# Two PSUM banks for the projections of the first part and of the last tail, and two sets of weight buffers in that tail

## Chip, core and metric

The kernel runs on one core of a Trainium2 chip. The metric is the device time of one execution in microseconds. Three executions of the kernel before gave 3626.5, 3629.08 and 3631.28 us; the median is 3629.08 us.

## The reference

One layer of a hybrid decoder for 1024 prompt tokens and 32 sample tokens, width 1024, in float32:

```python
z = rms_norm(x) @ W_in                   # 28 column chunks of 128: q,k,v of A; q,f,i,g of B
oa = dilated_attention(qa, ka, va)       # group A: 8 heads x 64
ob = hgrn2_chunked(qb, logf, kb, ib, s0) # group B: 4 heads x 128, gated
x += concat[rms_norm(oa), ob * silu(gb)] @ W_out
x += cross_attention(rms_norm(x), mk, mv, w_cq, w_co)   # 256 memory tokens
q = rms_norm(x) @ w_pq                   # 8 heads x 2 halves x 128: 16 column chunks
v1, i1 = top_k(q1 @ k1.T, 16); v2, i2 = top_k(q2 @ k2.T, 16)
sc, ci = top_k(all sums v1 + v2, 16);  e = i1[..] * 128 + i2[..];  g = softmax(sc)
a = gelu(x . peer_u[e]);  x += (g * a) @ peer_v[e]       # 16384 experts, 16 per head
y = rms_norm(x)
```

## The kernel before

**Products.** A float32 product is made of three matmuls of split operands (`mm3`, L201 to L203: high by high, high by low, low by high). `project` takes one PSUM bank, runs `mm3` over the input chunks into it and evacuates it. Weights come through `load_w`: two buffers for a projection with 1024 inputs (`kc` 8), one for one with 512, from a tag with three buffers. The first use of a weight splits it and stores it to DRAM (`wd_*`); later parts load the split form, 512 KB to a buffer, from the SP queue.

**Parts.** The 8 prompt tiles of 128 tokens and the sample tile (number 8) are worked through in three parts: tiles 0, 1, 2, then 3, 4 and the sample, then 5, 6, 7. Part 0 also carries the sample's 32 columns through its projections (416 columns). Each part has `z` (28 projections with `w_in`, each 24 matmuls into bank `z`, weights in `wz`), the attention and the recurrence that use them, and a `tail`: `w_out` (8 chunks), `w_cq` (4), cross attention, `w_co` (8, of 512 inputs) and `w_pq` (16), each `w_pq` chunk followed by the products with the expert keys (L674) and `top16` on VectorE (L917 to L921). The tails of parts 0 and 1 use the tag set "T" (weights `wt`, bank `y`), run beside the next part's middle, and are not changed. The tail of part 2 uses the set "Z" (weights `wz`, bank `z`), and runs beside `gates` 3 and 4, which build the dense gate matrix (L1024 to L1036).

**Experts.** Tiles 0 to 4 go through all 16384 experts densely: 128 iterations, each with the product of activations and the `u` block (bank `a`, L201 to L203), gelu (L1088), the product with the gates `gt` (L1090), its split (L170) and the products with the `v` block (L1098 to L1100). Inputs of the first iteration are `xh` and `xl` (eight loads, L1047), `gt` (L1064) and `u`. Tiles 5, 6, 7 and the sample gather their expert rows instead: GpSimd issues an indirect DMA per row (L1183), VectorE makes the dot product (L1190) or adds the row (L1201). Their indices come out of `select_tile` (L932 to L988) for the three tiles of part 2, called here a pick; the picks stand in the program between the first dense iterations. At the end stand the final norms (L1138 to L1153), the sample's last, which loads the sample's sum back (`u<-accd`).

**Order.** The Tile framework's scheduler makes one static order for each engine from the program, its buffers and its own estimate of durations; each engine runs its order strictly. A change of a buffer's name can thus move instructions anywhere on all engines. Where tiles live is decided by the allocation: the second dense gate buffers (`gt`, its third slot) lie on the same SBUF bytes as the `wt` buffers.

Of the kernel before, what the change touches and what calls it, by code (L numbers as in the profile page):

```python
# [64 lines left out]
def _body(tc, nc, ctx, A, O):  # L65
    V, S, PE, G, SP, ANY = nc.vector, nc.scalar, nc.tensor, nc.gpsimd, nc.sync, nc.any
# [23 lines left out]
    def T(p, shape, dt=F32, tag=None, bufs=None):  # L90
        seq[0] += 1
        kw = {} if bufs is None else {"bufs": bufs}
        if p is wk:
            p = wl if tag in LONG else wr if tag == "res" else we
        return p.tile(shape, dt, name=f"{tag}_{seq[0]}", tag=tag, **kw)

    def bank(tag="m"):
        return T(ps, [128, 512], F32, BANKS[tag], PB.get(BANKS[tag], 1))
# [69 lines left out]
    def split(hi, lo, src):  # L168
        S.copy(hi, src)  # L169
        V.tensor_tensor(lo, src, hi, op=ALU.subtract)  # L170
# [10 lines left out]
    def load_w(name, c, kc, tag, keep=True):  # L181
        out = []
        for i in range(kc // 4):
            w = T(wk, [128, 2, 4, 128], F32R, tag, 3)
            if (name, c, i) in wd:
                SP.dma_start(w.bitcast(F32), wd[name, c, i])
            else:
                raw = T(wk, [128, 4, 128], F32, "raw", 2)
                SP.dma_start(raw, A[name][c][:, 4 * i : 4 * i + 4])
                split(w[:, 0], w[:, 1], raw)  # L190
                if keep:
                    wd[name, c, i] = T(dr, [128, 2, 4, 128], F32, f"wd_{name}_{c}_{i}")
                    SP.dma_start(wd[name, c, i], w.bitcast(F32))
            out.append((w[:, 0], w[:, 1]))
        return out

    def mm3(out, w, x, kc, sl):
        xhi, xlo = x
        for c in range(kc):
            whi, wlo = (y[:, c % 4] for y in w[c // 4])  # L200
            PE.matmul(out, lhsT=whi, rhs=xhi[:, c, sl], start=c == 0, stop=False)  # L201
            PE.matmul(out, lhsT=whi, rhs=xlo[:, c, sl], start=False, stop=False)  # L202
            ins = PE.matmul(out, lhsT=wlo, rhs=xhi[:, c, sl], start=False, stop=c == kc - 1)  # L203
        return ins
# [18 lines left out]
    def hi_lo(g):  # L223
        return T(wk, [128, 8, g["xw"]], F32R, g["hi"]), T(wk, [128, 8, g["xw"]], F32R, g["lo"])

    def norm_T(src, n, g, bc, x, own=False):
        for c in range(8):
            s = src(c)
            t = s if own else T(wk, [128, WQ], F32, "t", TB)[:, :n]
            V.scalar_tensor_tensor(t, s, col(par, g + c), bc[:, :n], op0=ALU.mult, op1=ALU.mult)  # L230
            split(x[0][:, c, :n], x[1][:, c, :n], t)
        return x

    def gain_T(src, n, g, x):
        for c in range(8):
            hi, lo = (y[:, c, :n] for y in x)
            S.activation(hi, src(c), AF.Copy, scale=col(par, g + c))
            V.scalar_tensor_tensor(lo, src(c), col(par, g + c), hi, op0=ALU.mult, op1=ALU.subtract)
        return x
# [58 lines left out]
    def part(pi):  # L298
# [12 lines left out]
        WZP, N, NT = width(zt), width(th), len(th)  # L311
# [6 lines left out]
        h = []  # L318
# [17 lines left out]
        def project(w, x, kc, n, evac, tag):  # L336
            p = bank(tag)[:, :n]
            ins = mm3(p, w, x, kc, slice(0, n))
            if pi:
                anchors.append(ins)  # L340
            evac(p)

        def z(chunk, dst, fn=None):
            w = load_w("w_in", chunk, 8, "wz")

            def evac(p):
                if fn is None:
                    ANY.tensor_copy(dst, p[:, :NP])
                else:
                    S.activation(dst, p[:, :NP], fn)  # L350
                if first:
                    ANY.tensor_copy(zs[:, chunk], p[:, NP:])

            project(w, h, 8, WZP, evac, "z")

        def turn(dst, src, tag="m"):
            p = bank(tag)
# [4 lines left out]
        def z_some(c, group):  # L362
            r = {}
            for k, tag in group:
                t = T(wk, [128, 1024 if tag == "kT" else WT], F32, tag)
                r[tag] = t
                o = c0 if tag == "kT" else 0
                if o:
                    SP.dma_start(t[:, :c0], kdr[c][:, :c0])
                z(4 * k + c, t[:, o : o + NP], {"hq": AF.Silu, "gs": AF.Silu, "f": AF.Sigmoid}.get(tag))  # L370
            return r
# [148 lines left out]
        def tail(g):  # L520
            g = TAGS[g]
            tb = lambda k: bank(g["bank"] + k)
            tq = lambda k: T(wk, [128, g["qw"]], F32, g["q"][k])
            tw = lambda shape, dt=F32: T(g["pool"], shape, dt, g["tw"], 2)
            c2 = lambda shape, dt=F32: T(g["pool"], shape, dt, g["c2"], PTB if g["c2"] == "PT" else 2)
            put = lambda name, kc, x, evac: [
                project(load_w(name, c, kc, g["w"]), x, kc, N, lambda p: evac(c, p), g["bank"] + "y")
                for c in range(A[name].shape[0])]
            if smp:
                p = tb("m")  # L530
# [6 lines left out]
            y = hi_lo(g)  # L537
# [26 lines left out]
            if smp:  # L564
                p = tb("m")
# [17 lines left out]
            for j in range(NB):  # L583
                sl = slice(j * 128, (j + 1) * 128)
                po = tb("o")
                for hp2 in range(2):
# [16 lines left out]
                    p = tb("m")  # L603
# [17 lines left out]
            if smp or any(t in DENSE for t, o, rows in th):  # L621
                bc = bcast(r, th, g["bank"] + "m", g["bc"])
                h3 = norm_T(lambda c: xr[:, c, :N], N, G_FFN, bc, hi_lo(g))
                rs = None
            else:
                h3 = gain_T(lambda c: xr[:, c, :N], N, G_FFN, hi_lo(g))
# [9 lines left out]
            for j, (t, o, rows) in enumerate(th):  # L636
                xn = tw([128, 1024])
                for q in range(2):
                    p = tb("m")
# [16 lines left out]
            o = 0  # L656
# [5 lines left out]
            for jc in range(16):  # L662
                if jc % 8 == 0:
                    keys = tw([128, 8, 128])
                    SP.dma_start(keys, A["keys"][:, jc : jc + 8])
                    if smp:
                        sc4 = T(wk, [128, 2, 128], F32, "sc4")
                q = tq(jc % 2)
                project(load_w("w_pq", jc, 8, g["w"]), h3, 8, N, lambda p: ANY.tensor_copy(q[:, :N], p),
                        g["bank"] + "y")  # L670
                p = tb("m")
                for j, (t, o, rows) in enumerate(th):
                    r0 = 32 * (jc // 2 % 4) if t == 8 else 0
                    PE.matmul(p[r0 : r0 + rows, j * 128 : (j + 1) * 128], lhsT=q[:, o : o + rows], rhs=keys[:, jc % 8],  # L674
                              start=True, stop=True)
                sco = tq(2 + jc % 2)[:, : NB * 128].rearrange("p (j n) -> p j n", n=128)
                ANY.tensor_copy(sco, p[:, :NP].rearrange("p (i n) -> p i n", n=128))
                for j in range(NB):
                    top16(sco[:, j], lists[j][0][:, jc], lists[j][1][:, jc])
                if smp:  # L680
                    r0 = 32 * (jc // 2 % 4)
                    ANY.tensor_copy(sc4[r0 : r0 + 32, jc % 2], p[r0 : r0 + 32, NP : NP + 128])
                    if jc % 8 == 7:
                        for s in range(2):
                            k = jc // 8 * 2 + s
                            top16(sc4[:, s], lists[NB][0][:, k], lists[NB][1][:, k])
                if jc % 4 == 3:
                    yield
# [227 lines left out]
    def top16(s, v, i):  # L916
        V.max(v[:, 0:8], s)  # L917
        V.max_index(i[:, 0:8], v[:, 0:8], s)
        V.match_replace(s, v[:, 0:8], s, -3e38)
        V.max(v[:, 8:16], s)  # L920
        V.max_index(i[:, 8:16], v[:, 8:16], s)  # L921
# [308 lines left out]
    def seq_of(*fs):  # L1230
        for f in fs:
# [3 lines left out]
            else:  # L1235
                yield

    p = [part(i) for i in range(3)]

    def ahead(q):  # L1240
# [13 lines left out]
    with tc.tile_pool(name="dn", bufs=1, reuse_waits="tile") as dn, \  # L1254
            tc.tile_pool(name="dps", bufs=1, space=PSUM, reuse_waits="tile") as dps:
        work = dense(dv, dn, dps)
        for f in picks:
            next(work)
            f()
        late.close()  # L1260
        more = ctx.enter_context(tc.tile_pool(name="more", bufs=1, side="right", reuse_waits="tile"))
        for _ in work:
            pass
        for t in [t for part in PARTS for t in sorted(part, reverse=True) if t not in DENSE]:
            gather_tile(t)
        finish_sample(dn, dps)
# [103 lines left out]
```

## Time and profile before

| | |
|---|---|
| median of three executions | 3629.08 us |
| the profiled execution's own time | 3627.68 us |
| its span in the trace | 3625.8 us |
| mean granted TensorE clock | 0.977 |
| moved by DMA | 1007.82 MB, mean 278 GB/s |

The profiled execution is 1.4 us under the median; 1.9 us of it lie outside the span. The first 1650 us or so are parts and tails, then come some 90 us in which the last tail ends and the dense stage starts, then the dense stage to about 3580 us, and the final norms. Engine shares over all of that say little on one place; the stretches below are read apart.

### The profile page before, as it was taken

The page shows a single profiled execution, that of the slowest core. Times are in us where ns is not written, and L with a number is a line of the kernel's source. Part 1 is how long each engine was busy: PE and PEld are TensorE (multiplying, and loading weights), DVE is VectorE, ACT ScalarE, POOL GpSimd, SP SyncE. Part 2 cuts the span into 40 slices and gives each one's busy share as a digit, 9 for nine tenths or more (in the row PEclk, how much of TensorE's full clock was granted, in tenths as well). Part 3 has the DMA queues.
Part 4 walks back from the last instruction along what each step waited for, and adds up shares of the span by engine and source line. Part 5 has one row for each costly group of instructions (what it writes and reads, how often), then busy time and mean ns, then how long its engine had stood idle before and what let it go on. Part 6 is the DMA issues. An engine that isn't in the chain of part 4 may idle for free.

```text
span 3625.8 us, 52725 instructions
## 1 busy us (share of the span) xinstructions
PE 3373.7 (93%) x19343; PEld 2912.4 (80%) x19343; DVE 2634.7 (73%) x5868; ACT 1220.6 (34%) x2282; POOL 1112.5 (31%) x871
## 2 busy tenths in 40 slices
PE   5999999999999889887799999999999999999994
PEld 4886776677887788777788998999888898988893
DVE  4443333243885687897888878988888898888997
ACT  4544344344434443431242222222222222222221
POOL 0000000000000000021316644656566565565555
PEclk9999999999999999898999999999999999999997
DMA  7667777656655485499659988999999999999998
GB/s 243 230 226 248 239 247 240 202 181 220 210 192 201 179 293 209 150 338 344 229 169 348 341 291 286 364 351 337 340 335 351 345 333 342 337 343 332 329 328 296
DMA packets 408514, 1007.82 MB, mean 278 GB/s; under 512 B 43968, under 2 KB 168896, under 8 KB 406848
## 3 DMA queue, kind: packets, MB, share of 16 engines
q1 hardware_dynamic: 288448, 568.20, 45.6%
q0 software_dynamic: 119808, 436.26, 33.0%
q8 instruction: 152, 2.49, 0.3%
q14 instruction: 106, 0.87, 0.1%
HBM read 866.01 MB, written 138.31 MB: 277 GB/s over the span
## 4 chain that ended last, share of the span: by engine, by line
PE 71%; DVE 10%; DMA 9%; issue 4%; ACT 3%; POOL 1%; SPq 1%; POOLq 0%; DVEq 0%; ACTq 0%
PE a L201 7%; PE a L203 7%; PE a L202 7%; PE y L1098 4%; PE y L1099 4%; PE y L1100 4%; PE z L201 4%; PE z L202 3%; PE z L203 3%; PE yr L1098 3%; PE yr L1099 2%; PE yr L1100 2%; PE y L201 2%; PE y L202 2%; PE y L203 2%
## 5 line engine op out<-in xcount | busy, mean ns | idle before, releaser
L1183 POOL DMA_INDIRECT row<-in_peer_u,ix x416 | 534.6, 1285 | 635.9 <-DVE dots L1190 347.6
L1183 POOL DMA_INDIRECT row<-in_peer_v,ix x416 | 543.1, 1306 | 412.1 <-DVE ha L1201 266.5
L201 PE MATMUL a<-xh,u 128*128 128x320 f32 x2048 | 636.8, 311 | 21.2 <-ACT w L1088 18.0
L203 PE MATMUL a<-xh,u 128*128 128x320 f32 x2048 | 634.5, 310 | 0.7 <-DVE u L170 0.7
L202 PE MATMUL a<-xl,u 128*128 128x320 f32 x2048 | 634.1, 310 | 0.0
L1201 DVE SCALAR_TENSOR_TENSOR ha<-row,dots,ha 128x1024 f32<-128x1024 f32 x416 | 533.0, 1281 | 22.2 <-DMA row<-in_peer_v,ix 17.8
L1190 DVE CUSTOM_DVE_ANT_0 row<-row,ha 128x1024 f32<-128x1024 f32 x416 | 497.9, 1221 | 39.5 <-DMA row<-in_peer_u,ix 39.5
L210 POOL TENSOR_TENSOR rs_r<-rs_m,mhalf 128x3 f32<-128x3 f32 (+2 forms) x25 | 23.4, 944 | 1369.7 <-DVE rs_m L208 1250.2
L1088 ACT ACTIVATE w<-a 128x320 f32<-128x320 f32 x256 | 111.6, 436 | 937.3 <-PE a L203 917.1
L201 PEld LDWEIGHTS a<-xh,u 128*128 128x128 f32 x2048 | 385.6, 188 | 40.5 <-ACT w L1088 25.8
L202 PEld LDWEIGHTS a<-xl,u 128*128 128x128 f32 x2048 | 385.7, 188 | 8.8
L203 PEld LDWEIGHTS a<-xh,u 128*128 128x128 f32 x2048 | 385.5, 188 | 2.8 <-DVE u L170 1.0
L201 PE MATMUL z<-zhi,wz 128*128 128x384 f32 (+2 forms) x928 | 330.4, 356 | 43.0 <-DMA wz<-wd_w_pq 16.2
L202 PE MATMUL z<-zlo,wz 128*128 128x384 f32 (+2 forms) x928 | 316.8, 341 | 3.4 <-DVE zlo L170 1.9
L203 PE MATMUL z<-zhi,wz 128*128 128x384 f32 (+2 forms) x928 | 314.0, 338 | 0.0
L1099 PE MATMUL y<-v,w 128*128 128x512 f32 x768 | 294.6, 392 | 0.0
L1098 PE MATMUL y<-v,w 128*128 128x512 f32 x768 | 269.6, 393 | 12.6 <-ACT v L169 11.2
L1100 PE MATMUL y<-v,w 128*128 128x512 f32 x768 | 264.5, 391 | 1.3 <-DVE w L170 1.2
L201 PEld LDWEIGHTS z<-zhi,wz 128*128 128x128 f32 x928 | 181.0, 195 | 87.3 <-issue 21.7
L1098 PE MATMUL yr<-v,w 128*128 128x512 f32 x512 | 201.8, 394 | 13.5 <-DVE ys L1127 11.7
L169 ACT CAST w<-w 128x320 fp32r<-128x320 f32 x256 | 117.8, 460 | 259.0 <-DVE w L1090 258.5
L1100 PE MATMUL yr<-v,w 128*128 128x512 f32 x512 | 199.9, 390 | 0.7 <-DVE w L170 0.7
(470 smaller groups left out, 6685.2 us busy)
## 6 DMA issues: line engine op xcount, KB each, us to landing
u<-in_uT SPq DMA_DIRECT2D x128, 512.0 KB, 7.0
v<-in_peer_v SPq DMA_DIRECT2D x128, 512.0 KB, 7.6
wz<-wd_w_in SPq DMA_DIRECT2D x112, 512.0 KB, 4.3
gt<-gtall SPq DMA_DIRECT2D x124, 320.0 KB, 10.8
wd_w_in<-wz SPq DMA_DIRECT2D x56, 512.0 KB, 3.2
gtall<-sg SPq DMA_DIRECT2D x34, 512.0 KB, 4.1
wd_w_pq<-wt SPq DMA_DIRECT2D x32, 512.0 KB, 3.1
wt<-wd_w_pq SPq DMA_DIRECT2D x32, 512.0 KB, 4.5
```

The lines of the kernel that those rows point to most:

```text
L169: S.copy(hi, src)
L201: PE.matmul(out, lhsT=whi, rhs=xhi[:, c, sl], start=c == 0, stop=False)
L202: PE.matmul(out, lhsT=whi, rhs=xlo[:, c, sl], start=False, stop=False)
L203: ins = PE.matmul(out, lhsT=wlo, rhs=xhi[:, c, sl], start=False, stop=c == kc - 1)
L210: G.tensor_tensor(r, m, mhalf[:, :n], op=ALU.pow)
L1088: S.activation(ga[:, lo:hi], pa, AF.Gelu)
L1098: PE.matmul(o, lhsT=wh[:, sl], rhs=vh[:, ds], start=start and q == 0, stop=False)
L1099: PE.matmul(o, lhsT=wh[:, sl], rhs=vl[:, ds], start=False, stop=False)
L1100: PE.matmul(o, lhsT=wl[:, sl], rhs=vh[:, ds], start=False, stop=stop and q == len(ws) - 1)
L1183: G.indirect_dma_start(out=row, out_offset=None, in_=tab, in_offset=bass.IndirectOffsetOnAxis(ap=col(ix, j), axis=0))
L1190: V.tensor_tensor_reduce(row, row, hn, 1.0, 0.0, op0=ALU.mult, op1=ALU.add, accum_out=col(dots, j))
L1201: V.scalar_tensor_tensor(acc, row, col(dots, j), acc, op0=ALU.mult, op1=ALU.add)
```

## The change

The 28 projections of part 0 take turns between bank `z` and bank `x` (which the kernel maps to the physical bank `g`, also used by the sample's attention). In the tail of part 2, odd chunks of `w_out`, `w_cq`, `w_co` and `w_pq` go to bank `o` instead of `z`, and their weights to the three buffers of `wt` instead of the three of `wz`. `wt` also serves part 1's tail, which ends first.

```diff
+        zn = [0]
+
         def z(chunk, dst, fn=None):
             w = load_w("w_in", chunk, 8, "wz")
...
-            project(w, h, 8, WZP, evac, "z")
+            zn[0] += 1
+            project(w, h, 8, WZP, evac, "z" if pi or zn[0] % 2 else "x")
...
+            by = lambda c: "o" if pi == 2 and c % 2 else g["bank"] + "y"
+            wtag = lambda c: "wt" if pi == 2 and c % 2 else g["w"]
             put = lambda name, kc, x, evac: [
-                project(load_w(name, c, kc, g["w"]), x, kc, N, lambda p: evac(c, p), g["bank"] + "y")
+                project(load_w(name, c, kc, wtag(c)), x, kc, N, lambda p: evac(c, p), by(c))
                 for c in range(A[name].shape[0])]
...
-                project(load_w("w_pq", jc, 8, g["w"]), h3, 8, N, lambda p: ANY.tensor_copy(q[:, :N], p),
-                        g["bank"] + "y")
+                project(load_w("w_pq", jc, 8, wtag(jc)), h3, 8, N, lambda p: ANY.tensor_copy(q[:, :N], p),
+                        by(jc))
```

Lines behind the first edit stand 2 or 3 further down in the changed kernel, those behind the tail's edits 5: L1090 is L1095 there.

What the order shows. TensorE, first projections of part 0 (`z_266` is the first chunk's bank, `g_308` the second's; a piece of the difference):

```order
 L203 MATMUL z_266<-zhi_201,wz_252 128x416
+L201 MATMUL g_308<-zhi_201,wz_294 128x416
+L202 MATMUL g_308<-zlo_202,wz_294 128x416
+L203 MATMUL g_308<-zhi_201,wz_294 128x416
+L201 MATMUL g_308<-zhi_201,wz_294 128x416
+L202 MATMUL g_308<-zlo_202,wz_294 128x416
+L203 MATMUL g_308<-zhi_201,wz_294 128x416
 L201 MATMUL z_266<-zhi_201,wz_252 128x416
+L201 MATMUL g_308<-zhi_201,wz_294 128x416
 L202 MATMUL z_266<-zlo_202,wz_252 128x416
```

The second chunk's matmuls now stand between the first's, which come as the pieces of the normed input do; before they followed the first's evacuation. The third begins where it did.

The SP queue ahead of the dense stage, before (`wz` are the last `w_pq` weights, `xh`, `xl`, `gt`, `u` the dense inputs):

```order
L1047 DMA xh_15700<-h3x_65_163 128x1280
L186 DMA wz_15220<-wd_w_pq_1_1475_6874 128x1024
L1047 DMA xl_15701<-h3x_66_164 128x1280
L1047 DMA xh_15700<-h3x_65_163 128x1280
L1047 DMA xl_15701<-h3x_66_164 128x1280
L174 DMA u_15732<-in_uT 128x1024
L186 DMA wz_15272<-wd_w_pq_0_1483_6931 128x1024
L1047 DMA xh_15700<-h3x_65_163 128x1280
L1064 DMA gt_15720<-gtall_165 128x5x64
L186 DMA wz_15274<-wd_w_pq_1_1486_6938 128x1024
```

And now, from the last of the eight activation loads on:

```order
L1052 DMA xh_15700<-h3x_65_163 128x1280
L1052 DMA xl_15701<-h3x_66_164 128x1280
L1052 DMA xh_15700<-h3x_65_163 128x1280
L1052 DMA xl_15701<-h3x_66_164 128x1280
L1069 DMA gt_15720<-gtall_165 128x5x64 x4
L1069 DMA gt_15725<-gtall_165 128x5x128 x4
L1069 DMA gt_15730<-gtall_165 128x5x128
L174 DMA u_15732<-in_uT 128x1024
L1069 DMA gt_15730<-gtall_165 128x5x128 x3
```

Seventeen of the 32 `w_pq` weight loads stood behind the first `xh` load before, and three `u` loads ahead of the last weights; now all 32 weights are ahead of the eight `xh` and `xl` loads, and every `u` load comes after. The four `gt_15725` loads go to the bytes of `wt` and wait for the last projection's matmuls, and the first `u` is queued behind them.

VectorE at the end, before, from the last sum of the dense stage on (`ys`, L1127; `ha_31808` is the last gathered tile, a row for each gathered expert):

```order
L1127 TENSOR_TENSOR ys_3269_15718<-ys_3269_15718,yr_29565 128x512
L1201 SCALAR_TENSOR_TENSOR ha_31808<-row_32160,dots_31423,ha_31808 128x1024
L1201 SCALAR_TENSOR_TENSOR ha_31808<-row_32163,dots_31423,ha_31808 128x1024
L1201 SCALAR_TENSOR_TENSOR ha_31808<-row_32166,dots_31423,ha_31808 128x1024
L1201 SCALAR_TENSOR_TENSOR ha_31808<-row_32169,dots_31423,ha_31808 128x1024
L1201 SCALAR_TENSOR_TENSOR ha_31808<-row_32172,dots_31423,ha_31808 128x1024
L1152 SCALAR_TENSOR_TENSOR u_29589<-u_29589,fst_29593,u_29598 128x1024
```

And now:

```order
L1132 TENSOR_TENSOR ys_3269_15718<-ys_3269_15718,yr_29565 128x512
L1153 TENSOR_SCALAR fst_29593<-fst_29593 128x1
L1206 SCALAR_TENSOR_TENSOR ha_31808<-row_32187,dots_31423,ha_31808 128x1024
L1206 SCALAR_TENSOR_TENSOR ha_31808<-row_32190,dots_31423,ha_31808 128x1024
L1206 SCALAR_TENSOR_TENSOR ha_31808<-row_32193,dots_31423,ha_31808 128x1024
L1157 SCALAR_TENSOR_TENSOR u_29589<-u_29589,fst_29593,u_29598 128x1024
```

Behind the last `ys` there were twelve gathered rows (to `row_32193`), and there are three now. At the start of the dense stage the move is the other way: the first product with the gates (L1090, now L1095) stood ahead of nearly all of the first pick's instructions on VectorE, and now stands behind all but a few of them; the split of the first `u` block (L170) stands behind most of that pick too.

## Rows read from the trace of the kernel before

**Rows 1.** The page, busy time, share of the span and instructions of each engine.

```profile
PE 3373.7 (93%) x19343; PEld 2912.4 (80%) x19343; DVE 2634.7 (73%) x5868; ACT 1220.6 (34%) x2282; POOL 1112.5 (31%) x871
```

**Rows 2.** Stretches: length, busy time of each engine, PEclk, DMA share, GB/s.

```profile
26.00:48.00 22.00, 11.08 (x24) 7.11 (x24) 12.35 (x25) 6.96 (x13) 0.00 (x0) 1.00 0.59 188
...
700.00:1100.00 400.00, 392.25 (x2287) 318.96 (x2285) 248.50 (x1063) 167.39 (x284) 5.26 (x6) 0.98 0.60 201
...
1420.00:1580.00 160.00, 133.05 (x847) 124.09 (x846) 140.89 (x441) 71.25 (x155) 12.66 (x12) 0.90 0.54 193
1580.00:1643.00 63.00, 52.23 (x347) 48.98 (x346) 61.99 (x137) 22.65 (x49) 14.10 (x12) 0.92 0.97 355
1643.00:1680.00 37.00, 27.95 (x147) 25.81 (x147) 32.51 (x176) 7.00 (x13) 5.62 (x6) 0.86 1.01 385
1680.00:1735.00 55.00, 41.19 (x214) 37.46 (x212) 36.99 (x180) 9.40 (x18) 8.56 (x10) 0.91 0.90 310
1735.00:1757.00 22.00, 6.37 (x37) 6.11 (x38) 14.59 (x50) 1.25 (x3) 5.86 (x6) 0.69 0.63 218
...
1900.00:3500.00 1600.00, 1573.50 (x8788) 1422.83 (x8787) 1375.32 (x1896) 413.66 (x680) 936.87 (x723) 1.00 0.93 335
```

**Rows 3.** Waits of TensorE to 310 us: total us, times, longest us.

```profile
PE z L201 <- ACT zhi L169: 9.6, 4, 3.6
PE z L201 <- ACT zs L352: 9.1, 9, 1.9
```

**Rows 4.** Waits of TensorE from 1580 to 1757 us.

```profile
PE z L201 <- DMA wz<-wd_w_pq: 16.2, 6, 6.0
PE a L201 <- ACT w L1088: 15.2, 1, 15.2
...
PE m L674 <- ACT aq L669: 3.1, 5, 0.6
```

**Rows 5.** Waits of VectorE from 1643 to 1757 us.

```profile
DVE vals L917 <- ACT hq L677: 14.0, 4, 6.7
DVE ha L1201 <- DMA row<-in_peer_v,ix: 7.4, 4, 4.4
```

**Rows 6.** DMA issues from 1640 to 1740 us: KB each, median us to landing.

```profile
wz<-wd_w_pq SPq DMA_DIRECT2D x21, 512.0 KB, 6.3
xh<-h3x SPq DMA_DIRECT2D x4, 640.0 KB, 12.1
...
gt<-gtall SPq DMA_DIRECT2D x8, 320.0 KB, 8.1
u<-in_uT SPq DMA_DIRECT2D x3, 512.0 KB, 12.3
```

**Rows 7.** Timeline: last gate input, last projection, first dense gelu (start, us).

```profile
1643.06 0.69 DVE L1024 TENSOR_TENSOR raw<-iota,x_vs 128x512 f32<-128x512 f32 x1
...
1734.43 0.34 PE L203 MATMUL z<-zhi,wz 128*128 128x384 f32 x1
...
1754.60 0.44 ACT L1088 ACTIVATE w<-a 128x320 f32<-128x320 f32 x1 [17.71 <-DVE ixb L949]
```

**Rows 8.** The first products with the gates: ns min/median/max, first and last start.

```profile
L1090 DVE TENSOR_TENSOR w<-w,gt x7: 472/492/496, 1757.5 to 1793.9; 128x320 f32<-128x320 f32 x7
```

**Rows 9.** VectorE from 1754.3 to 1815 us, of the first pick: total us, mean ns.

```profile
L960 DVE TENSOR_TENSOR tw<-tw,ixb 128x2048 bf16<-128x2048 bf16 x2 | 2.5, 1226 | 0.0
L958 DVE TENSOR_TENSOR tw<-tw,iota 128x2048 bf16<-128x2048 bf16 x2 | 2.4, 1202 | 0.0
...
L921 DVE FIND_INDEX8 ci<-sc,tw 128x8 uint16<-128x100 f32 x8 | 2.0, 258 | 0.0
```

**Rows 10.** Timeline of VectorE at the end.

```profile
3581.36 0.68 DVE L1127 TENSOR_TENSOR ys<-ys,yr 128x512 f32<-128x512 f32 x1
...
3602.17 1.28 DVE L1201 SCALAR_TENSOR_TENSOR ha<-row,dots,ha 128x1024 f32<-128x1024 f32 x1 [1.46 <-DMA row<-in_peer_v,ix]
```

**Rows 11.** GpSimd and VectorE from 3540 us on: busy us, mean ns, idle before.

```profile
L1183 POOL DMA_INDIRECT row<-in_peer_v,ix x29 | 35.5, 1223 | 16.0 <-DVE ha L1201 9.3 <-issue 4.6 <-DVE fst L1148 1.4
```

**Rows 12.** The chain that ended last, after the last gathered row: start, us.

```profile
3606.98 0.31 DMA u<-accd
...
3621.15 1.27 DVE u L1152
```

## The prediction

> **What bounds the kernel now.** The page's first part says TensorE, at 93% [rows 1], but that is an average. The table of stretches [rows 2] shows where it holds: from 700 to 1100 us TensorE is busy 392.25 of 400 us and in the dense stage 1573.5 of 1600, so time saved ahead of such a stretch is kept and time saved on another engine inside it is not. It does not hold in part 0's first projections (11.08 of 22 us from 26 to 48 us), from 1420 to 1643 us, where VectorE is busy 140.89 of 160 and then 61.99 of 63 us, nor from 1643 to 1757 us, where TensorE has 27.95 + 41.19 + 6.37 = 75.5 of 114 us, VectorE 32.51 + 36.99 + 14.59 = 84.1, and the DMA engines stand at 1.01 and 0.90. Those are the places of the change. I then read the waits of TensorE and VectorE in these stretches, the landing times of the loads there, and the timeline around the first dense iteration and the end.
>
> **Part 0.** The change adds no instruction of weight; it takes away the wait of a projection's first matmul for the evacuation of the one before. That wait is listed: 9.1 us in nine pieces for the sample's piece `zs` [rows 3], the last that reads the bank. With two banks the evacuation of one projection has the whole of the next to hide under, and I take 5 of the 9.1 us, because some of the gaps lie where the inputs or the work of the attention come late too. The other part is the head. The first projection waits for the pieces of the normed input, 9.6 us in four waits [rows 3], and TensorE is half idle there [rows 2]. The order puts the second projection's matmuls between them, so up to one projection lies in those gaps. It is 24 matmuls, but issued while input pieces still come, and the third starts no earlier in the order; I take 5. Together -10. Bounds: nothing of the head and half of the waits, -4; all of both, 9.1 and some 6, -15. The sample's attention, which shares bank `g`, is pushed back behind the last even projection. It is filler between projections and is not on the path unless it delays part 1's start; TensorE at 98% afterwards [rows 2] means that its work costs the same at either place, so I cost that at nothing. If that cover is gone, it is in the bound of -4.
>
> The Trainium skill, Perfetto Trace Analysis, Optimizing Tensor Performance (Matmuls), says that independent groups should rotate through PSUM banks so that an evacuation overlaps the next group. The `zs` row agrees for part 0; for the tail the rule would promise a gain per projection that the rows of that tail do not offer, since evacuation is not what the projections wait for there.
>
> **The last tail, to 1643 us.** Here VectorE is the full engine [rows 2], by the gates and `top16`. Neither bank nor weights make its work less: 0, between -3 and +3, since odd `w_out` chunks now wait until part 1's tail frees `wt`.
>
> **From 1643 us to the dense stage.** The gates end with the last `raw` at 1643.06 us, the last projection's last matmul stands at 1734.43 us [rows 7], the first product with the gates at 1757.5 us [rows 8]: 91 and 114.5 us after the gates. TensorE waits 16.2 us for the `w_pq` weights, in six waits, and 3.1 us for `aq` [rows 4]; VectorE waits 14.0 us for `hq` [rows 5], the score that comes late for the same reason. With six buffer sets and all weights ahead of the dense inputs in the queue, those waits go. TensorE's own work from the gates' end to the last projection is 27.95 + 41.19 = 69.1 us [rows 2], so that projection can end about 91 - 69 = 22 us earlier, perhaps 27.
>
> What is late next decides. First the loads. The eight `xh`/`xl` loads of 640 KB, the `gt` loads and the first `u` now come after all weights; part of `gt` waits for the last projection, as its bytes are those of `wt`. Eight x loads are 5.2 MB, 13.6 us at the 385 GB/s of the fullest stretch [rows 2]; they are issued with the last weights, some three projections (12 us) before that end. Behind the last projection come about 2 MB of `gt` and the first `u`, 6 to 7 us at that rate, and landing took 12.3 us for `u` [rows 6]. So the first `a` matmul could start some 20 us behind the last projection, at 69 + 20 = 89 us after the gates, still well ahead of 114.5.
>
> Second VectorE. Its 84.1 us until the first product held almost none of the first pick. Now nearly the whole pick stands ahead. Priced by its rows, each of five passes over eight heads is about 2 us (the row of 8 in 2.0), with value loads about 10; two masks and two products at 1.2 us make 4.9 [rows 9]; the smaller ones some 6: about 21 us. Five gathered rows fewer stand ahead (36 instead of 41 by the order), 6 us at 1.28 [rows 10]. So 84 + 21 - 6, about 99 us of work. The idle part was 114.5 - 84.1 = 30 us; without the 14.0 us for `hq` and with the rows' 7.4 us still there [rows 5], I take 8 to 16 us, so the first product comes at 107 to 115 us, on the mean 3 us earlier than before. Third, the dense stage starts with fewer `u` blocks at hand (three were loaded ahead before); with 12.3 us of landing [rows 6] against an iteration of some 14.2 us (128 of them from 1757.5 to 3581.36 us [rows 8, 10]), a late block costs part of one: I take 6 us for the first ones. Together +3. Bounds: the weights' gain kept to half, -10; VectorE idle by as much as before, 99 + 30 = 129 us, +15, and with late `u` blocks +18.
>
> A rule speaks for more: the Trainium skill, DMA: Bandwidth & Descriptors, Rules for kernel authors, advises to issue a load early and wait late. By it the 16.2 us would be gained whole, and the sum would be some 3592 us. By the DMA share of 1.01 beside it [rows 2], the early weights take the place of the dense inputs on the same engines. I keep the rows.
>
> **The end.** After the dense stage's last sum (`ys`, 3581.36 us) twelve gathered rows were still to be added, the last at 3602.17 us [rows 10]: 20.8 us, 1.7 us each, which is near GpSimd's rate (29 issues in 35.5 us busy and 16 us idle, 1.8 us each [rows 11]). Behind that come the norms and the sample, which is loaded back at 3606.98 us and ends 18 us later [rows 12]. With pick 1 done earlier the gather runs ahead by about ten rows, and three are left behind `ys` by the order. Nine rows at 1.7 us would be 15; the dense tiles' own norms (about 10 us of VectorE) then decide, so I take -12. Bounds: -16, and -5 if the gather falls behind its order because its loads stay as slow (DMA share 0.93 [rows 2]).
>
> **Sum.** Against the profiled execution's 3627.68 us: -10 + 3 - 12 = -19, so 3608.7. That execution stands 1.4 us under the median of the runs shown; I say 3609.
>
> **Rivals.**
> First, slower. The prologue on VectorE is exposed: pick 1, the rest of `top16` and some twenty gather operations stand in front of the first `u` split and the first product, in strict order, and each gathered row waits for its DMA just while x, `gt` and `u` (9 MB, 23 us at 385 GB/s) are on the same engines. Then the idle part is 30 + 23 us, the first product at 99 + 53 = 152 us after the gates, +37. With -10 of part 0 and the end's gain down to -14 at best, it is +13: 3641. It decides from about +29 on, that is from a first product later than 143 us after the gates. For it speaks that TensorE already waits 15.2 us for the first gelu [rows 4], which waited 17.71 us [rows 7]; against it that no row wait there was over 4.4 us [rows 5].
> Second, no change. The gather keeps its old pace, so the end gives nothing, and the prologue takes back what part 0 gave: -10 + 8 + 0, about 3626. The full DMA engines speak for it.
> Third, more. The early weights' gain also survives: -10 - 16 - 10, about 3592. It needs a VectorE that is not idle in those 99 us and loads of x that land before the last projection. The `hq` wait of 14.0 us speaks for it, the pick in front against.
> Fourth, the change does not do what it says in part 0, where the waits for `zs` turn into waits for `zhi` or weights: -2 there, and the rest as forecast, about 3617, which is still on the forecast's side.
>
> **Chances.** Forecast (3598 to 3621, with the fourth) 0.50; more, 0.13; no change 0.18; slower 0.19. About 0.2% (7 us) is what a measurement of this kernel can tell from no change. Faster holds the forecast, the third and a little of the second's lower edge: 0.64; same 0.18; slower 0.18. The range leaves out the outer parts of the third and of the first case: 3582 to 3640.
>
> **What would show it.** Part 0: the `zs` row of TensorE's waits gone, the start of part 1's work 10 us earlier. The tail: the row of waits for `wz<-wd_w_pq` below 5 us, the last projection about 69 us after the last `raw`; the first product with the gates at 107 to 115 us after it; no more than 6 us lost in the first dense iterations. The end: three additions behind the last `ys`, and from that `ys` to `u<-accd` about 13 us instead of 25.6. Wrong would be a dense stage that starts far later after the gates than before, or rows that lag behind the order, so that the additions wait for DMA after the last `ys`.

## The result, and the profile after

The changed kernel takes 3607.57 us (median of 6 runs, 3600.23 to 3615.01), the kernel before 3631.61 us in runs beside it (6 runs, 3626.5 to 3639.34). The ratio is 0.9933, with a 95% interval of 0.992 to 0.9947: faster by 24 us. The forecast was 3609 us. The profiled execution's span is 3606.0 us against 3625.8 before, 19.8 us less.

The page of the changed kernel, its first part, and its table of stretches, cut at the same events as the one below it (28th projection of part 0 evacuated, end of the last part's recurrence, last gate input, first product with the gates, last dense sum); columns as in [rows 2]:

```profile
PE 3384.5 (94%) x19343; PEld 2918.3 (81%) x19343; DVE 2631.9 (73%) x5874; ACT 1221.4 (34%) x2276; POOL 1108.5 (31%) x871
```

```profile
26.00:48.00 22.00, 16.71 (x48) 11.78 (x48) 13.83 (x27) 7.94 (x16) 0.00 (x0) 0.80 0.71 227
48.00:91.00 43.00, 42.98 (x235) 36.92 (x236) 22.23 (x63) 28.97 (x66) 0.00 (x0) 0.95 0.68 228
91.00:287.00 196.00, 185.75 (x1097) 165.71 (x1095) 89.80 (x263) 105.55 (x229) 2.70 (x4) 0.97 0.72 249
287.00:1183.00 896.00, 882.75 (x5003) 659.91 (x5003) 438.26 (x1634) 371.25 (x679) 13.42 (x16) 0.98 0.65 215
1183.00:1624.30 441.30, 385.89 (x2624) 356.81 (x2623) 370.02 (x1091) 182.86 (x446) 28.21 (x25) 0.95 0.69 244
1624.30:1734.00 109.70, 65.51 (x373) 63.13 (x371) 99.71 (x499) 20.31 (x31) 17.71 (x18) 0.78 0.84 292
1734.00:3573.50 1839.50, 1799.33 (x9960) 1622.66 (x9960) 1577.63 (x2261) 488.67 (x786) 1040.35 (x797) 0.99 0.90 325
3573.50:3606.00 32.50, 3.80 (x4) 0.36 (x4) 15.11 (x21) 5.67 (x11) 4.21 (x6) 0.53 0.59 193
```

The kernel before, cut at those events (its first stretch stands in [rows 2]):

```profile
48.00:91.00 43.00, 38.73 (x188) 33.57 (x188) 19.78 (x55) 25.75 (x55) 0.00 (x0) 1.00 0.71 235
91.00:308.00 217.00, 204.25 (x1187) 174.11 (x1187) 92.31 (x269) 108.79 (x241) 3.24 (x4) 0.98 0.68 229
308.00:1200.00 892.00, 869.33 (x5002) 656.94 (x5002) 442.89 (x1643) 370.90 (x680) 13.23 (x15) 0.99 0.65 217
1200.00:1643.00 443.00, 382.22 (x2590) 356.09 (x2589) 369.84 (x1101) 181.74 (x443) 29.82 (x26) 0.93 0.66 237
1643.00:1757.50 114.50, 76.01 (x398) 69.88 (x398) 84.59 (x408) 17.66 (x33) 20.17 (x22) 0.85 0.88 317
1757.50:3581.40 1823.90, 1786.48 (x9953) 1613.37 (x9951) 1581.20 (x2326) 492.93 (x791) 1028.66 (x787) 1.00 0.90 323
3581.40:3625.80 44.40, 3.80 (x4) 0.36 (x4) 26.39 (x29) 5.63 (x10) 15.46 (x13) 0.52 0.68 249
```

Read the differences between the cuts. Part 0's last projection is 21 us earlier (308 to 287), the end of the last recurrence 17 us (1200 to 1183), the last gate input 18.7, the first product with the gates 23.5 (1757.5 to 1734.0). Then the dense stage is 15.6 us longer (1839.5 against 1823.9), though its work is the same, and the end 11.9 us shorter (32.5 against 44.4). In sum 23.5 - 15.6 + 11.9 = 19.8.

The waits of part 0 (TensorE to 310 us, as in [rows 3]):

```profile
PE z L201 <- ACT zhi L169: 4.7, 4, 1.7
...
PE z L201 <- ACT zs L354: 1.1, 1, 1.1
```

The waits for the bank's evacuation fell from 9.1 to 1.1 us, those for the normed input from 9.6 to 4.7, and idle time of TensorE from 26 to 91 us fell from 10.9 + 4.3 to 5.3 + 0.0 us. From 26 us to the end of part 0 it fell from 27.9 to 15.6 us, by 12.4. The other 8.6 of the 21 us are work that is no longer done ahead of that event: TensorE's busy time up to it is shorter by so much.

The last tail and the start of the dense stage: TensorE's longest wait from 1560 to 1757 us, a wait of ScalarE from 1620 to 1740 us, the last projection's last matmul, the last gate input, and the first products with the gates (as in [rows 4, 7, 8]):

```profile
PE a L201 <- ACT u L169: 24.6, 1, 24.6
```

```profile
ACT c L972 <- DVE c L971: 16.2, 1, 16.2
```

```profile
1680.48 0.33 PE L203 MATMUL o<-zhi,wt 128*128 128x384 f32 x1
```

```profile
1624.34 0.68 DVE L1029 TENSOR_TENSOR raw<-iota,x_vs 128x512 f32<-128x512 f32 x1
```

```profile
L1095 DVE TENSOR_TENSOR w<-w,gt x7: 483/491/493, 1734.0 to 1771.0; 128x320 f32<-128x320 f32 x7
```

No wait of TensorE for `w_pq` weights is left in that stretch; the first dense matmul now waits 24.6 us for the split of the first `u` block on ScalarE. ScalarE comes to that split behind the exponential of the first pick (`c`, L972), for which it waits 16.2 us until VectorE has got that far. The last projection ends 56 us after the last gate input, before 91, and the first product comes 109.7 us after it, before 114.4.

The end, VectorE, and the load of the sample's sum (its first and last start is the last pair of numbers):

```profile
3573.46 0.68 DVE L1132 TENSOR_TENSOR ys<-ys,yr 128x512 f32<-128x512 f32 x1
...
3574.12 3.91 DVE L1206 SCALAR_TENSOR_TENSOR ha<-row,dots,ha 128x1024 f32<-128x1024 f32 x3
```

```profile
L1215 SPq DMA_DIRECT2D u<-accd x1: 732/732/732, 3586.5 to 3586.5; - x1
```

Three rows in one go without a wait, where twelve with waits stood [rows 10]; the sample's sum is loaded 13.0 us after the last `ys`, before 25.6.

### The profile page after: what moved, and what is told of

Read it like the earlier page. It is cut to its first block, busy times and chain, and to the rows that moved or that the text cites. A ratio compares the mean times of both kernels' runs of the same rounds, so it can differ in the third digit from the quotient of the medians.

```text
span 3606.0 us, 52703 instructions
## 1 busy us (share of the span) xinstructions
PE 3384.5 (94%) x19343; PEld 2918.3 (81%) x19343; DVE 2631.9 (73%) x5874; ACT 1221.4 (34%) x2276; POOL 1108.5 (31%) x871
## 4 chain that ended last, share of the span: by engine, by line
PE 73%; DVE 9%; DMA 9%; issue 4%; ACT 2%; POOL 1%; SPq 0%; POOLq 0%; DVEq 0%; ACTq 0%
PE a L201 7%; PE a L203 7%; PE a L202 7%; PE y L1103 4%; PE y L1104 4%; PE y L1105 4%; PE z L201 3%; PE z L202 3%; PE z L203 3%; PE yr L1103 3%; PE yr L1104 2%; PE yr L1105 2%; PE y L201 2%; DMA u<-in_uT 2%; PE y L202 2%
## 5 line engine op out<-in xcount | busy, mean ns | idle before, releaser
L201 PE MATMUL a<-xh,u 128*128 128x320 f32 x2048 | 640.0, 313 | 47.1 <-ACT u L169 35.3
L1103 PE MATMUL y<-v,w 128*128 128x512 f32 x768 | 300.5, 392 | 6.4 <-ACT w L169 6.4
L1104 PE MATMUL y<-v,w 128*128 128x512 f32 x768 | 300.4, 392 | 0.0
L1105 PE MATMUL y<-v,w 128*128 128x512 f32 x768 | 248.0, 390 | 1.6 <-DVE w L170 1.6
L201 PE MATMUL z<-zhi,wz 128*128 128x384 f32 (+2 forms) x688 | 237.9, 346 | 8.3 <-ACT zhi L169 4.7
L202 PE MATMUL z<-zlo,wz 128*128 128x384 f32 (+2 forms) x688 | 230.5, 335 | 1.9 <-DVE zlo L238 1.2
L203 PE MATMUL z<-zhi,wz 128*128 128x384 f32 (+2 forms) x688 | 227.6, 331 | 0.0
L1103 PE MATMUL yr<-v,w 128*128 128x512 f32 x512 | 204.3, 399 | 9.7 <-DVE ys L1132 9.3
L1104 PE MATMUL yr<-v,w 128*128 128x512 f32 x512 | 202.6, 396 | 0.0
L1105 PE MATMUL yr<-v,w 128*128 128x512 f32 x512 | 202.0, 394 | 0.0
```

The source lines that it names most:

```text
L1103: PE.matmul(o, lhsT=wh[:, sl], rhs=vh[:, ds], start=start and q == 0, stop=False)
L1104: PE.matmul(o, lhsT=wh[:, sl], rhs=vl[:, ds], start=False, stop=False)
L1105: PE.matmul(o, lhsT=wl[:, sl], rhs=vh[:, ds], start=False, stop=stop and q == len(ws) - 1)
```

## Experiments

Events read from one traced execution each, in us: 28th projection of part 0 evacuated (P0), end of the last part's recurrence (R), first product with the gates (W), length of the dense stage (D) and time in it at the low clock, half of the full one (L, without a stretch that was already running at W, which is up to 5 us), from the last dense sum to the end (E), and gathered rows left behind that sum by the order (n). Executions of one kernel differ by up to 7 us at R and 9 us in D, and its times by 9 us or more, so differences of a few us between rows say little.

```
                          P0      R       W       D       L     E     n
before                   307.8  1199.7  1757.5  1823.9   0.0  44.5   12
before, again            310.7  1206.4  1763.2  1823.9   3.4  44.8   12
the change               286.9  1183.4  1734.0  1839.5  27.3  32.5    3
the change, again        286.7  1184.1  1732.4  1830.8  15.6  33.6    3
the change, third        286.5  1183.5  1732.0  1837.9  23.9  33.3    3
part 0 alone             283.7  1175.0  1730.6  1839.7  23.9  43.2   13
second projection alone  302.5  1186.3  1745.1  1824.6   7.0  39.6   10
part 0 without second    291.7  1196.0  1747.7  1833.7  10.2  39.3   10
last tail alone          306.7  1202.7  1751.7  1836.6  20.5  32.9    3
tail: banks only         280.9  1177.0  1723.3  1830.6  13.7  40.8   11
tail: weights only       283.0  1180.8  1772.4  1818.3  11.7  22.4    0
tail: w_pq only          281.8  1182.4  1738.3  1835.5  19.8  29.8    0
w_pq weights in one set  286.6  1184.9  1729.0  1826.3   3.4  38.0    9
the same, again          284.4  1183.1  1733.6  1834.1  18.7  37.1    9
```

**Part 0 alone.**

```diff
-            by = lambda c: "o" if pi == 2 and c % 2 else g["bank"] + "y"
-            wtag = lambda c: "wt" if pi == 2 and c % 2 else g["w"]
+            by = lambda c: g["bank"] + "y"
+            wtag = lambda c: g["w"]
```

> Only part 0's projections alternate between two banks; the last tail is as before. Theory A (each place pays its own part, and TensorE's full stretches carry it on): the 28th projection of part 0 is evacuated about 21 us earlier than before, the last gate input about 15 us, and the end is about 15 us earlier: ratio near 0.996. Rival B (part 0's gain is taken back at the last tail, where VectorE is full, and the whole gain of the change comes from the tail's order): same early gain, but the end within 5 us of before, ratio 0.999 or more.

Ratio to the kernel before 0.9958 (0.9944 to 0.9971), 15 us faster. Theory A holds; B, that the last tail takes it back, does not: W is 27 to 33 us earlier than in the two executions before. Half of that is lost again in the traced execution's dense stage, which is 15.8 us longer.

**The last tail alone.**

```diff
-            project(w, h, 8, WZP, evac, "z" if pi or zn[0] % 2 else "x")
+            project(w, h, 8, WZP, evac, "z")
```

> Only the last tail alternates (banks and weights); part 0 is as before. Theory A: the time from the last gate input to the first product with the gates falls by about 5 us, the time from the last dense sum to the end by about 12 us, and the dense stage may give some back: in all 5 to 12 us faster, ratio 0.997 to 0.9985. Rival B (all of the gain is the tail's): 20 us faster, ratio 0.9945. Rival C (the late dense inputs cost what the order at the end gives): within 4 us of before.

Ratio 0.9973 (0.9957 to 0.9988), 10 us faster. Theory A holds; B and, narrowly, C lie outside the interval. With the 15 us of part 0 alone that makes 25, the change's own 24: the two halves add up. The end is 32.9 us as in the change, so that part of the gain is the tail's.

**The tail's banks without the weights.**

```diff
-            wtag = lambda c: "wt" if pi == 2 and c % 2 else g["w"]
+            wtag = lambda c: g["w"]
```

> As the change, but the last tail's weights all stay in the three wz buffers; only its banks alternate. Theory A (in the tail the weights count, not the banks, since evacuation was only waited for some 3 us): like part 0 alone, within 4 us of it, and the waits for w_pq weights stay at about 16 us. Rival (the bank is what holds the tail back): like the whole change, about 22 us faster than before.

Ratio 0.9928 (0.9908 to 0.9947): as fast as the whole change, and 12 us faster than part 0 alone on the same chip (3604.82 against 3616.52 us). Theory A falls here, and TensorE's waits for `w_pq` weights were 5.7 us and not some 16; two banks are enough for this tail's gain. Whether it is the evacuation itself that is hidden, or the order that the scheduler makes with two banks, is not separated: in this kernel the last gate input stands at 1662.7 us, 38 us later than in the change, and the first product follows it after 60.6 us.

**The tail's weights without the banks.**

```diff
-            by = lambda c: "o" if pi == 2 and c % 2 else g["bank"] + "y"
+            by = lambda c: g["bank"] + "y"
```

> As the change, but the last tail keeps bank z alone; its weights alternate between wz and wt. Theory A: within 4 us of the whole change (about 22 us faster than before), waits for w_pq weights nearly gone. Rival (the second bank is needed to use the weights that have come early): 10 us or more slower than the whole change.

Ratio 0.9979 (0.9962 to 0.9996). The rival holds: it is 17 us slower than the whole change. Beside part 0 alone it gains nothing; its median is 9 us longer (3625.18 against 3616.52 us), but the intervals of the two ratios overlap. W is 42 us later than with part 0 alone, the end 21 us shorter and the dense stage 21 us shorter, so that the traced execution, one of the fastest of this kernel (3614.93 us), is as long as the one with part 0 alone. Which term makes the median longer is not shown. Where the start goes, ScalarE's waits from 1600 to 1775 us and TensorE's groups from 1700 to 1790 us (busy, mean ns, idle before):

```profile
ACT f L682 <- DVE vals L926: 27.3, 5, 8.2
ACT hq L682 <- DVE vals L926: 25.6, 6, 6.8
ACT c L972 <- DVE c L971: 21.3, 1, 21.3
```

```profile
L201 PE MATMUL a<-xh,u 128*128 128x320 f32 x35 | 13.0, 372 | 37.1 <-ACT u L169 35.3 <-ACT w L1093 1.9
```

`ACT c L972` is the exponential of the first pick. ScalarE stands 21.3 us in front of it, until VectorE has got that far in the pick; the split of the first `u` block comes behind it in ScalarE's order, and TensorE stands 35.3 us for that split. This is the first rival of the prediction, the pick ahead of the dense stage, at nearly its price: the first product comes 154 us after the last gate input (1618.2 us), where the rival had 152. It does not bring the rival's time of 3641 us, since the end is 22 us shorter than before where the rival had 14 at best, and the dense stage 6 us shorter.

**Which projection of part 0.** First only the second one to the other bank, then all but the second (both with the two lines of part 0 alone, which leave the tail as before):

```diff
-            project(w, h, 8, WZP, evac, "z" if pi or zn[0] % 2 else "x")
+            project(w, h, 8, WZP, evac, "x" if not pi and zn[0] == 2 else "z")
```

> Only the second projection of part 0 goes to the other bank; all else is as before. Theory (the head gives some 8 us, the rest of the projections some 13): evacuation of the 28th projection about 8 us earlier than before, at 300 us. Rival (the head's gain is lost to later waits for inputs): within 2 us of before, 306 to 308 us.

```diff
-            project(w, h, 8, WZP, evac, "z" if pi or zn[0] % 2 else "x")
+            project(w, h, 8, WZP, evac, "z" if pi or zn[0] % 2 or zn[0] == 2 else "x")
```

> Part 0's projections alternate, but the second stays in bank z behind the first; the tail is as before. Theory: evacuation of the 28th projection about 13 us earlier than before, at 295 us. Rival (all of the gain comes from the head): 306 us or more.

P0 is 302.5 and 291.7 us, 5 to 8 and 16 to 19 us earlier than in the two executions before: both pieces exist and add up to about the change's 21 to 24. What is left of them at R does not follow that split: 13 to 20 us with the second projection alone, 4 to 10 with the rest. Each of these kernels has its own order between P0 and R. Nor do the times follow it, with one execution of each on one chip: 3611.17 us with the second projection alone, 3622.95 with the rest, 3598.91 with the whole change, 3635.41 and 3633.72 before. A single projection on the other bank came out 22 to 24 us faster there; single executions of these kernels spread too far to price it.

**The same two kernels again.**

> The kernel before, once more. If the dense stage's length is set by its matmuls and by how often the granted clock falls to half there, then its length is 1824 us plus half of the time at the low clock, whatever that is in this execution; if the change's own order made the dense stage longer, then this one is again near 1824 us with no stretch at the low clock.

> The changed kernel, once more. As for the kernel before: dense stage 1824 us plus half of its time at the low clock, or, if the order is the cause, again about 1839 us with some 27 us at the low clock. The last dense sum to the end again 32 to 33 us, the gates' end to the first product again 108 to 112 us.

The dense stage of these two and of the change's third execution:

```profile
1763.20:3587.10 1823.90, 1787.18 (x9953) 1614.91 (x9951) 1581.78 (x2326) 492.60 (x791) 1030.88 (x787) 1.00 0.91 323
```

```profile
1732.40:3563.30 1830.90, 1794.74 (x9960) 1617.78 (x9958) 1577.24 (x2262) 488.82 (x786) 1028.60 (x797) 1.00 0.91 326
```

```profile
1732.00:3569.90 1837.90, 1798.48 (x9960) 1622.35 (x9960) 1577.62 (x2261) 488.51 (x786) 1032.59 (x797) 0.99 0.91 325
```

The changed kernel was at the low clock for 15.6 to 27.3 us of its dense stage, the kernel before for 0 and 3.4 us, and TensorE's busy time grew by 8 to 13 us, about half of that. Length and low clock go together: 1824 us plus half of L is within 5 us of D in all rows of the table but one (tail: weights only, 12 us below it), which is the first theory; the rival's dense stage of about 1839 us did not come in the change's second execution. It is not a proof of the cause: the waits that go before the low clock cost time too, and no run changed the one without the other.

**Only `w_pq` alternates in the tail, and all but the `w_pq` weights.**

```diff
-                project(load_w(name, c, kc, wtag(c)), x, kc, N, lambda p: evac(c, p), by(c))
+                project(load_w(name, c, kc, g["w"]), x, kc, N, lambda p: evac(c, p), g["bank"] + "y")
```

> As the change, but in the last tail only w_pq alternates (banks and weights); w_out, w_cq and w_co are as before. Theory A2 (the w_pq weights from six buffers push the dense inputs and the first u back, and let the pick go ahead of the dense stage): the first product with the gates is late, 107 us or more after the last gate input, at 1734 us or later; no gathered row is left behind the last dense sum by the order, so from there to the end it takes 22 to 23 us; in all within 8 us of the change. Rival (what w_out, w_cq and w_co gain is what makes the change fast): 10 us or more slower than the change.

```diff
-                project(load_w("w_pq", jc, 8, wtag(jc)), h3, 8, N, lambda p: ANY.tensor_copy(q[:, :N], p),
+                project(load_w("w_pq", jc, 8, g["w"]), h3, 8, N, lambda p: ANY.tensor_copy(q[:, :N], p),
```

> As the change, but the w_pq weights stay in wz; banks alternate everywhere in the last tail, and so do the weights of w_out, w_cq and w_co. Theory A2: like the kernel in which only banks alternate: the first product with the gates at 1722 to 1732 us (before the change's 1732 to 1734), from the last dense sum to the end 38 to 40 us, nine rows being left there by the order; ratio 0.992 to 0.994. Rival (any weights in wt cost the early start): first product at 1734 us or later.

Ratios 0.9916 (0.9894 to 0.9938) and 0.9898 (0.9881 to 0.9915). With `w_pq` alone the start is late as expected, W 1738.3, though 105 us and not 107 or more after the last gate input; no row is left behind the last sum, as expected, but the end took 29.8 us and not 22 to 23, for which the runs give no reason. With the `w_pq` weights in one set W is 1729.0 us, 3 to 5 us earlier than the change's, and the end 5 us longer; in the second execution W is 1733.6, no earlier than the change's. The ratio came out below the 0.992 to 0.994 expected. That kernel seemed the faster by this, so it and the change were timed beside each other:

> The changed kernel, timed on the same chip as the kernel whose w_pq weights stay in one set: about 0.9933 of the kernel before. If the early w_pq weights cost the dense stage's start more than they save at its end, it is slower than that kernel by 3 to 12 us; if the two ends cancel, the two are within 3 us.

> The kernel whose w_pq weights stay in wz, once more, beside the changed kernel: 0.990 of the kernel before, 3 to 12 us faster than the changed kernel; dense stage 1824 us plus some 0.6 us for each us at the low clock.

3608.72 us (0.9927, 0.9898 to 0.9956) and 3607.28 us (0.9918, 0.9888 to 0.9947). The 3 to 12 us expected between the two are not there, and they are not told apart; there is no version here that is shown to beat the change.

## Why the prediction was right, point by point

**Part 0: the mechanism was right, its size too small.** The head was put at 5 us; TensorE's idle time from 26 to 48 us fell by 5.6, and the kernel with the second projection alone shows 5 to 8. Of the 9.1 us of `zs` waits 8 went, where 5 were forecast. Up to P0 TensorE's idle time fell by 12.4 us, which is near the -10. What failed is the step "TensorE at 98% afterwards [rows 2] means that its work costs the same at either place, so I cost that at nothing". From P0 to R TensorE's idle time also fell, from 892.0 - 869.3 = 22.7 to 896.0 - 882.75 = 13.3 us: the order behind part 0 leaves fewer holes. That the sample's attention, moved back, fills them is not shown: with the second projection alone as many matmuls (1402) start ahead of P0 as before, and 16.5 us are idle from P0 to R. So the term was -10, and at R it measures 16 to 23 us over the executions; -15 us of time for the kernel with part 0 alone. The five other kernels with this part 0 and another tail reach R at 1175.0 to 1184.9 us, so some of what R shows hangs on the rest of the order.

**The last tail to the gates' end: 0 forecast, 2 to 3 us gained, within its bounds.** From R to the last gate input the kernel before needs 443.4 and 443.9 us, the change 440.5 to 441.2. But the tail as a whole, from R to W, gained 6 to 10 us where 3 were forecast (556.8 and 557.8 us before, 548.3 to 550.6 in the change), and the kernel with the tail's banks beside part 0 alone gains 12 us of time. From R to W it needs 546.3 us, part 0 alone 555.6. The Trainium skill's rule on rotating banks (Perfetto Trace Analysis, Optimizing Tensor Performance) was set aside for this tail because the wait rows there were short; the run with the banks agrees with the rule there too in that two banks gain, and does not show that it is by the overlap of evacuations that the rule names.

**From the gates to the dense stage: right.** The first product was put at 107 to 115 us after the last gate input; it came after 109.7, 107.8 and 107.3 us. VectorE was busy for 99.7 of the 109.7 us, where 99 us of work and 8 to 16 idle were forecast. Two steps on the way were off and did not count: the last projection came 56 us after the last gate input and not 69, and the first dense matmul 99 us after it and not 89, held by the split of `u` and not by loads. That what is late next is VectorE with the pick ahead of the first `u` shows in the 24.6 us of TensorE's wait for that split and the 16.2 us of ScalarE's wait ahead of it; without a second bank they are 35.3 and 21.3 us. By the Trainium skill's advice to issue loads early (DMA: Bandwidth & Descriptors, Rules for kernel authors) the 16.2 us of waits for weights would have been gained whole; here those waits went and another took their place, the early weights alone gained nothing over part 0 alone, and with both banks the early `w_pq` weights made no difference that the runs tell (0.9927 with them, 0.9918 without, side by side).

**The first dense iterations: the 6 us were the wrong place and too small.** The dense stage lost 7 to 16 us. Its first seven products with the gates take 37.0 us against 36.4 before [rows 8], so it is not lost at the start. TensorE is busy for 12.9 us more in the profiled execution and idle for 2.8 us more; the loss goes with stretches at the low clock around short waits, which the forecast did not have. It is the term that took back what the stages ahead of it gave more than forecast: in the profiled execution, -23.5 to the first product against -13 forecast (its -10 and the -3 of the first product), +15.6 in the dense stage against +6.

**The end: right.** -12 forecast, 11.9 measured; 13.0 us from the last `ys` to `u<-accd`, about 13 forecast. Over the fourteen executions E falls with n: 43 to 45 us at 12 and 13, 37 to 41 at 9 to 11, 32 to 34 at 3, 22 to 30 at 0.

So the total of 3609 us stands 1 us from the measured 3607.57, and the gain of 24 us beside the 20 forecast, partly because two misses, 10 us too little ahead of the dense stage and 10 too little in it, cancel. That the total came so near is luck; the direction and the end are not. The forecast's last step has a slip as well: 3608.7 and the 1.4 us by which that execution stood under the median make 3610, not 3609.

The rivals: the slower one's late start is real, but only with the weights alone, and even there the kernel is not slower than before; no change and the whole gain of the early weights are out, and so is the fourth, since the `zs` waits went and the `zhi` waits fell too. What stays open is why the changed kernel's dense stage has more of the waits that go with the low clock. One, of 2.5 to 3.6 us at about 2149 us, recurs in all three of its executions and has no counterpart of 1 us or more in the two before, so it may belong to the new order. The one that ends at 3294 us, for the 110th `u` block, is not new: TensorE waits there for the same block in the kernel before, for 2.0 and 3.0 us in its two executions against 5.3, 2.6 and 1.1 us. What makes that block late was not tried.

## What to carry to other kernels

Ahead of a stretch where one engine is full, a second bank can be worth more than the wait rows of one projection say, as here, where the order behind it closed up too; count the idle time to the next fixed event and not only the named wait. More buffers for a stream of loads change what stands ahead of what on the queue and on the other engines: look for what the early loads let the scheduler put in front of the next stage. Where a tail of leftover work follows a long stage, the number of items left behind the stage's last instruction can be read from the order and prices the end to within some 5 us.

## What the runs showed of the hardware

In the dense stage, most waits of TensorE of two to six microseconds (some 33 of 46 over the fourteen traced executions) had a stretch of some three to seven microseconds at a granted clock of half behind them or beginning within them. One place in the changed kernel, stretches and timeline of TensorE:

```profile
3270.00:3288.00 18.00, 18.00 (x97) 16.05 (x97) 13.40 (x23) 2.66 (x5) 10.16 (x9) 1.00 1.00 357
3288.00:3294.00 6.00, 0.84 (x4) 0.38 (x2) 0.69 (x1) 0.94 (x1) 0.00 (x0) 0.82 0.84 336
3294.00:3300.00 6.00, 5.85 (x18) 4.84 (x19) 3.98 (x5) 1.15 (x2) 0.95 (x1) 0.61 0.35 103
3300.00:3318.00 18.00, 17.47 (x106) 16.04 (x105) 15.62 (x23) 4.91 (x9) 11.26 (x8) 1.00 0.79 274
```

```profile
3288.00 0.39 PE L1105 MATMUL yr<-v,w 128*128 128x512 f32 x1
...
3294.15 0.64 PE L201 MATMUL a<-xh,u 128*128 128x320 f32 x1 [5.31 <-ACT u L169]
...
3295.28 0.63 PE L1104 MATMUL yr<-v,w 128*128 128x512 f32 x1
```

The clock falls within the wait of 5.31 us (0.82 on the mean of its 6 us), and it is 0.61 on the mean of the next 6 us, that is the level of 1.2 GHz for most of them; a matmul of 512 columns lasts 0.63 us instead of 0.39 there, and 18 matmuls are done where 6 us held some 32 before. So by these rows such a wait costs its own length and then, as an estimate, some 3 us more. In the first execution of the kernel before, no wait in the dense stage, the longest of them 2.1 us, was followed by this:

```profile
3300.24 0.42 PE L201 MATMUL a<-xh,u 128*128 128x320 f32 x1 [2.02 <-ACT u L169]
```

```profile
3300.00:3306.00 6.00, 5.06 (x30) 4.58 (x31) 5.78 (x9) 0.63 (x2) 2.84 (x2) 1.00 0.37 120
```

The length of a wait alone does not decide it: in the changed kernel's first execution a wait of 2.03 us at 3172 us was followed by the low clock, and in its third one a wait of 3.63 us at 2205 us was not.
